# Two groups of Strassen differences, from VectorE to GpSimd, in a two-layer network

## The chip, the cores and the metric

The kernel is one program on one core of a Trainium2 chip. The metric is the device time of one execution in microseconds (us). The core has engines that run their own instruction queues and meet at semaphores: TensorE (PE in the profile; PEld is its weight load) multiplies matrices into PSUM, VectorE (DVE) does elementwise work and reductions, ScalarE (ACT) does activations, casts and copies, GpSimd (POOL) does elementwise work too, and SyncE (SP) issues the DMAs here. SBUF and PSUM are the on-chip memories; HBM holds inputs, outputs and what is put by.

## The reference

Two layers over 1024 tokens of width 1024, in float32. Layer 0 mixes tokens by sliding-window attention with sinks, layer 1 by a gated recurrence (HGRN2); each is followed by an MLP with squared ReLU and a hidden width of 4096, and a last RMS norm ends the network:

```python
for layer in range(DEPTH):
    h = rmsnorm(x, mix_norm[layer])
    y = sliding_window_attention(h, ...) if layer % 2 == 0 else hgrn2_recurrence(h, ...)
    x = x + y
    h = rmsnorm(x, mlp_norm[layer])
    x = x + jnp.square(jax.nn.relu(h @ w_up)) @ w_down
return rmsnorm(x, final_norm)
```

In layer 1 `h @ w_in` gives four projections (q, f, i, g), each 1024 x 1024.

## The kernel before

**Layout.** Activations are held transposed: 8 tiles of 128 features (`kt`), each with two halves of 512 tokens (`hf`). A tile is 128 partitions by 512 float32 columns. Tiles are named by tag: `a` (60 buffers), `t` (18), `m` (6), raw weights `wr` (6), split weights `wh` and `wl` (5 each), and the PSUM banks `p` and `q` (4 each). The profile gives these tags as names, with buffer numbers left out.

**Precise products.** Each operand of a matrix product is split into a high part, rounded to fp32r by a cast on ACT (`a<-t` or `wh<-wr`), and the rest, a subtraction on VectorE (`a<-t,a` or `wl<-wr,wh`). `mm3` (line 491) makes three matmuls of them. Both tiles of a split must be there before TensorE can use them.

**Strassen.** The first projection of a layer is computed in seven products instead of eight. With u the operand tiles of the first token half and q01, q11 those of the second half (lower and upper features), the seven operands are: 1 and 2 the halves of u (`begin`, line 647), 5 = q01 - u_j, 3 = q11, 6 = q11 - (5), 7 = q11 - q01, and 4 = u_(j+4) - (6). `finish` (line 656) makes operands 5, 3, 6, 7 and 4, four tiles each, and splits them all. The stored u tiles come back from HBM by DMA into `t` tiles (`stored`). `finish` is called three times: at the end of layer 0's attention for that layer's MLP (`mlp_second`, line 705), before the recurrence's projections (`hgrn`, line 1792), and before layer 1's MLP. Products that need operands 1 and 2 alone (`pair_first`, `two_first`) are begun ahead, so that TensorE has work while `finish` runs; after them come 5, 6, 3, 7, 4 in the MLP and 5, 6, 7, 3, 4 in the recurrence, 12 matmuls each.

**The order of the work.** Nothing is issued as it is written. `Schedule.add` records every operation with its reads, its writes, the engines that may run it and a cost for each. `order` (line 358) then runs a list scheduler over the whole program: `forward` gives each engine its operations in order, by their rank, with buffers handed out as they come free; `backward` works out from the end how late each may be, which becomes its rank; four passes are made and the one with the shortest modelled time is issued. Each engine then runs its own order strictly. The model charges latencies between engines (`LATENCY`). Elementwise operations on two tiles go through `tt` (line 470):

```python
cost = {"DVE": 70 + n * 1.04 + more, "Pool": 147 + n * 2.105}
engines = ("DVE",) if e == "any" else (e,)
```

So `"any"` means VectorE, and `"Pool"` means GpSimd, where the model charges 147 + 512 x 2.105 = 1225 ns for a tile. The model has no term for two engines that use the same memory ports. All instructions are issued through one closure, so the profile gives line 433 for every one of them and groups must be told apart by tile names and time. GpSimd has, before the change, memsets and small copies in the attention, a few small operations in the recurrence and two multiplications in the last norm.

Of the kernel before, what the change touches and what calls it, by code (L numbers as in the profile page):

```python
# [14 lines left out]
ALU = mybir.AluOpType  # L15
# [363 lines left out]
class Net:  # L379
# [276 lines left out]
    def finish(self, which, upper_first=False, keep=False):  # L656

        x, t, q01, q11 = self.b, [], [], []
        self.u3, self.u5 = [], []

        def stored(j):
            z = self.t()
            self.dma(z, self.u[j], 4 * P * TH)
            return z

        def lower():
            for j in range(HK):
                q01.append(self.gained(which, j, 1))
                t.append(stored(j))
                self.tt("any", t[j], q01[j], t[j], ALU.subtract)  # L670
                x[5].append(self.split(t[j]))
                if keep:
                    self.u5.append(self.keep(t[j]))

        def upper():
            for j in range(HK):
                q11.append(self.gained(which, j + HK, 1))
                x[3].append(self.split(q11[j]))
                if keep:
                    self.u3.append(self.keep(q11[j]))  # L680

        for part in (upper, lower) if upper_first else (lower, upper):
            part()
        for j in range(HK):
            self.tt("any", t[j], q11[j], t[j], ALU.subtract)
            x[6].append(self.split(t[j]))
        for j in range(HK):
            self.tt("any", q01[j], q11[j], q01[j], ALU.subtract)
            x[7].append(self.split(q01[j]))
        self.u4 = []  # L690
        for j in range(HK):
            z = stored(j + HK)
            self.tt("any", z, z, t[j], ALU.subtract)
            x[4].append(self.split(z))
            if keep:
                self.u4.append(self.keep(z))
        return x
# [1233 lines left out]
```

## Time and profile before

| what | value |
|---|---|
| median of 3 runs | 2050.66 us (2050.44 to 2050.85) |
| the profiled execution | 2050.68 us |
| its span, first to last instruction | 2048.9 us |
| TensorE clock granted | 0.999 of full |
| busy PE, DVE, ACT, POOL | 2037.5, 1854.9, 1306.6, 57.3 us |
| HBM read and written | 394.57 and 100.14 MB |

Busy time is the union of an engine's instruction times. Matmuls overlap each other and their ends are modelled, so a busy TensorE is not a TensorE at its peak; how many matmuls fall into a window says more. A row of a timeline has the start and the length in us, the engine, the line, the operation, the tiles it writes and reads, the shapes, how many alike are merged, and in brackets the idle time before and what ended it. A duration of a VectorE row includes some 0.08 us in which the next one already runs. Rows of the chain of waits have start, length and what the chain ran through.

### The profile page before, as it was taken

To read this page: it belongs to the slowest core of one execution; us is meant where nothing else is said; L and a number is where in the kernel's file an instruction comes from. 1 tells how busy PE (TensorE), PEld (TensorE's weight loads), DVE (VectorE), ACT (ScalarE), POOL (GpSimd) and SP (SyncE) were. 2 spreads that over 40 slices of the span, in tenths; PEclk is the share of its full clock that TensorE was granted. 3 is DMA by queue.
4 is the path that set the end of the run, shared out by engine and by line. 5 is a ranking of instruction groups with operands and counts; after the bars stand their busy time and mean duration, and the time that the engine had idled before them with its cause. 6 is when DMAs were issued, how large, how long until landed. Compare 5 with 4: busy or idle time off the path is not lost.

```text
span 2048.9 us, 36889 instructions
## 1 busy us (share of the span) xinstructions
PE 2037.5 (99%) x12300; PEld 1740.4 (85%) x12300; DVE 1854.9 (91%) x3751; ACT 1306.6 (64%) x2711; POOL 57.3 (3%) x120
## 2 busy tenths in 40 slices
PE   9999999999999999999999999999999999999998
PEld 8878888899998888888888888888889999888887
DVE  8899979899999979889988889999999899997985
ACT  7577976667675544657665556666767677544573
POOL 4030000000000000000000000000000000000000
PEclk9999999999999999999999999999999999999999
DMA  6212378788789977665777788988798788997712
GB/s 227 78 52 73 134 262 270 234 273 287 262 291 312 319 264 255 214 205 198 267 267 267 264 272 286 322 287 301 246 297 293 271 286 285 323 323 238 267 52 83
DMA packets 275407, 497.19 MB, mean 243 GB/s; under 512 B 30992, under 2 KB 36368, under 8 KB 275216
## 3 DMA queue, kind: packets, MB, share of 16 engines
q1 hardware_dynamic: 275072, 494.81, 71.6%
q8 instruction: 97, 1.59, 0.3%
q14 instruction: 94, 0.77, 0.1%
q10 hardware_dynamic: 144, 0.02, 0.0%
HBM read 394.57 MB, written 100.14 MB: 241 GB/s over the span
## 4 chain that ended last, share of the span: by engine, by line
PE 93%; DVE 4%; DMA 1%; issue 1%; ACT 0%; SPq 0%; DVEq 0%
PE p L433 50%; PE q L433 44%; DVE t L433 1%; DVE a L433 1%; DVE wl L433 1%; DMA a<-in_wg 1%; DMA a<-in_x 0%; DVE m L433 0%; DVE sm L433 0%; SPq L433 0%; DMA c<-in_sinks 0%; ACT m L433 0%; ACT a L433 0%; DVE c L433 0%; ACT t L433 0%
## 5 line engine op out<-in xcount | busy, mean ns | idle before, releaser
L433 PE MATMUL p<-a,wh 128*128 128x512 f32 (+1 forms) x2832 | 779.4, 360 | 0.3 <-DVE a L433 0.2
L433 PE MATMUL q<-a,wh 128*128 128x512 f32 x2020 | 625.5, 390 | 0.0
L433 PEld LDWEIGHTS p<-a,wh 128*128 128x128 f32 x2832 | 503.0, 189 | 79.6 <-DVE a L433 1.3
L433 PE MATMUL p<-a,wl 128*128 128x512 f32 (+1 forms) x1416 | 503.5, 358 | 0.4 <-DVE wl L433 0.4
L433 PEld LDWEIGHTS q<-a,wh 128*128 128x128 f32 x2020 | 374.9, 188 | 73.8 <-ACT a L433 0.2
L433 PE MATMUL q<-a,wl 128*128 128x512 f32 x1008 | 392.1, 389 | 0.0
L433 ACT CAST wh<-m 128x512 fp32r<-128x512 f32 (+1 forms) x354 | 213.4, 607 | 195.8 <-PE q L433 100.0
L433 ACT CAST wh<-wr 128x512 fp32r<-128x512 f32 (+1 forms) x324 | 194.9, 604 | 172.5 <-PE p L433 104.6
L433 PEld LDWEIGHTS p<-a,wl 128*128 128x128 f32 x1416 | 266.0, 189 | 38.4 <-DVE wl L433 1.1
L433 DVE TENSOR_TENSOR wl<-m,wh 128x512 fp32r<-128x512 f32 (+1 forms) x354 | 234.4, 668 | 37.5 <-ACT wh L433 31.6
L433 DVE TENSOR_TENSOR a<-t,a 128x512 fp32r<-128x512 f32 (+2 forms) x321 | 211.2, 674 | 18.8 <-PE q L433 7.8
L433 DVE TENSOR_TENSOR wl<-wr,wh 128x512 fp32r<-128x512 f32 (+1 forms) x324 | 214.3, 665 | 15.3 <-ACT wh L433 13.5
L433 DVE TENSOR_TENSOR t<-t,t 128x512 f32<-128x512 f32 (+3 forms) x376 | 218.5, 601 | 9.5 <-ACT t L433 7.1
L433 PEld LDWEIGHTS q<-a,wl 128*128 128x128 f32 x1008 | 189.3, 188 | 39.2
L433 ACT ACTIVATE t<-t 128x512 f32<-128x512 f32 x288 | 179.5, 631 | 58.7 <-DVE t L433 47.6
L433 ACT CAST a<-t 128x512 fp32r<-128x512 f32 (+1 forms) x241 | 143.2, 607 | 24.2 <-DVE t L433 9.5
L433 DVE TENSOR_TENSOR t<-t,p 128x256 f32<-128x256 f32 x288 | 115.9, 414 | 15.0 <-PE p L433 11.2
L433 PE MATMUL p<-wh,a 128*128 128x512 f32 x384 | 125.9, 397 | 0.3 <-DVE a L433 0.3
L433 DVE TENSOR_TENSOR m<-wr,wr 128x512 f32<-128x512 f32 (+1 forms) x184 | 118.8, 648 | 0.3
L433 ACT COPY t<-q 128x512 f32<-128x512 f32 (+2 forms) x174 | 95.7, 556 | 20.6 <-PE q L433 16.1
L433 DVE TENSOR_TENSOR a<-a,a 128x512 fp32r<-128x512 f32 (+2 forms) x151 | 100.8, 679 | 7.7 <-ACT a L433 3.2
L433 ACT CAST a<-a 128x512 fp32r<-128x512 f32 x136 | 82.7, 619 | 25.8 <-DVE a L433 21.8
(135 smaller groups left out, 2535.9 us busy)
## 6 DMA issues: line engine op xcount, KB each, us to landing
t<-d SPq DMA_DIRECT2D x592, 256.0 KB, 4.6
a<-d SPq DMA_DIRECT2D x318, 256.0 KB, 4.2
d<-t SPq DMA_DIRECT2D x290, 256.0 KB, 3.3
wr<-in_down SPq DMA_DIRECT2D x224, 256.0 KB, 4.2
wr<-in_up SPq DMA_DIRECT2D x172, 256.0 KB, 4.3
wr<-in_win SPq DMA_DIRECT2D x68, 256.0 KB, 4.1
d<-a SPq DMA_DIRECT2D x64, 256.0 KB, 3.3
wr<-in_wqkv SPq DMA_DIRECT2D x48, 256.0 KB, 3.0
```

The lines of the kernel that those rows point to most:

```text
L433: fn(*[place(a) for a in args], **{k: place(v) for k, v in kw.items()})
```

## The change

In `finish` the four differences that make operand 7 and the four that make operand 4 go to GpSimd instead of VectorE. Their casts, their splits, the differences of operands 5 and 6 and all else are as before; the scheduler makes its plan anew with these costs. As `finish` runs three times, 24 operations move.

```diff
             self.tt("any", t[j], q11[j], t[j], ALU.subtract)
             x[6].append(self.split(t[j]))
         for j in range(HK):
-            self.tt("any", q01[j], q11[j], q01[j], ALU.subtract)
+            self.tt("Pool", q01[j], q11[j], q01[j], ALU.subtract)
             x[7].append(self.split(q01[j]))
         self.u4 = []
         for j in range(HK):
             z = stored(j + HK)
-            self.tt("any", z, z, t[j], ALU.subtract)
+            self.tt("Pool", z, z, t[j], ALU.subtract)
             x[4].append(self.split(z))
             if keep:
                 self.u4.append(self.keep(z))
```

## The prediction

> **What bounds the kernel now.** I read the page first, then the groups by line, then the chain of waits, and last windows and timelines at the three places where the edited lines run. Two groups and the totals:
>
> ```profile
> span 2048.9 us, 36889 instructions
> PE 2037.5 (99%) x12300; PEld 1740.4 (85%) x12300; DVE 1854.9 (91%) x3751; ACT 1306.6 (64%) x2711; POOL 57.3 (3%) x120
> PE 93%; DVE 4%; DMA 1%; issue 1%; ACT 0%; SPq 0%; DVEq 0%
> ...
> L433 DVE TENSOR_TENSOR t<-t,t 128x512 f32<-128x512 f32 (+3 forms) x376 | 218.5, 601 | 9.5 <-ACT t L433 7.1 <-PE q L433 0.6
> L433 POOL TENSOR_TENSOR a<-a,t 128x512 f32<-128x512 f32 x2 | 2.6, 1302 | 689.0 <-DVE a L433 677.6 <-ACT t L433 11.4
> ```
>
> TensorE bounds the kernel (99% busy, 93% of the chain), VectorE is next at 91%, and GpSimd has nearly nothing. GpSimd has done the operation in question twice in this program: 1302 ns each. Every line has the number of one helper (L433), so the stages must be found by time. `finish` runs three times: before layer 0's MLP (300 to 332 us), before the recurrence's projections (912 to 944) and before layer 1's MLP (1418 to 1458). Windows there (length; busy time and count of PE, PEld, DVE, ACT, POOL; clock; DMA):
>
> ```profile
> 300.00:332.00 32.00, 32.00 (x147) 26.60 (x146) 31.39 (x54) 24.19 (x43) 0.00 (x0) 1.00 0.86 278
> 360.00:376.00 16.00, 16.00 (x72) 13.28 (x71) 10.13 (x20) 9.83 (x19) 0.00 (x0) 1.00 0.76 245
> 912.00:944.00 32.00, 31.76 (x144) 25.91 (x143) 31.83 (x53) 21.86 (x39) 0.00 (x0) 1.00 0.38 136
> 940.00:945.00 5.00, 4.39 (x18) 2.78 (x17) 5.00 (x9) 1.11 (x2) 0.00 (x0) 1.00 0.16 54
> 1418.00:1458.00 40.00, 40.00 (x177) 32.72 (x176) 39.53 (x67) 35.87 (x64) 0.00 (x0) 1.00 0.81 284
> ```
>
> VectorE is full in all three: 31.39 of 32, 31.83 of 32, 39.53 of 40 us. What differs is how close TensorE is behind it. In the second place it already waits. The chain of waits there, and its usual step for 12 matmuls:
>
> ```profile
> 316.14 2.72 PE p L433 x12
> ...
> 929.27 10.71 PE p L433 x48
> 939.99 0.60 DVE t L433
> 940.59 0.60 DVE wl L433
> 941.19 0.60 DVE a L433
> 941.79 0.60 DVE t L433
> 942.39 1.20 DVE a L433 x2
> 943.60 0.60 DVE t L433
> ```
>
> A matmul takes 2.72 / 12 = 0.227 us. The 18 of 940 to 945 account for 18 x 0.227 = 4.08 us, so TensorE stands idle for 0.92 us; the chain runs on VectorE because the fourth operand's splits (the two `a` at 942.39) come too late. In the other two places the last split of the fourth operand (VectorE) and the first matmul that reads it (TensorE) are these, first stage, then third:
>
> ```profile
> 331.87 0.69 DVE L433 TENSOR_TENSOR a<-t,a 128x512 fp32r<-128x512 f32 x1 [0.33 <-ACT a L433]
> 339.37 0.62 PE L433 MATMUL q<-a,wh 128*128 128x512 f32 x2
> 1456.76 0.69 DVE L433 TENSOR_TENSOR a<-t,a 128x512 fp32r<-128x512 f32 x1
> 1457.68 0.39 PE L433 MATMUL q<-a,wh 128*128 128x512 f32 x1
> ```
>
> Its reader in the first stage is the second matmul of that row, at 339.37 + 0.23 = 339.60: 7.0 us after 331.87 + 0.69 = 332.56. In the third stage 1457.68 - 1457.45 = 0.23 us are left. So VectorE has 7 us to spare in the first stage, 0.2 in the third, and none in the second.
>
> **The change part by part.** Removed from VectorE: in each stage four differences q11 - q01 for the seventh operand and four z - t for the fourth, 24 in all. Each is a `t<-t,t` over 512 columns and frees one step of VectorE's queue, 0.60 us by two consecutive rows:
>
> ```profile
> 1441.11 0.69 DVE L433 TENSOR_TENSOR a<-t,a 128x512 fp32r<-128x512 f32 x1
> 1441.71 0.69 DVE L433 TENSOR_TENSOR t<-t,t 128x512 f32<-128x512 f32 x1
> ```
>
> That is 8 x 0.60 = 4.8 us less per stage. Nothing else is removed; casts, splits, loads and TensorE's work stay, and no DMA is issued anew or past another.
>
> Added on GpSimd: 8 x 1.30 = 10.4 us per stage. Its queue is empty there (its instructions before and after the second stage):
>
> ```profile
> 853.76 0.18 POOL L433 IOTA t<- 128x64 int32 x1 [615.81 <-PE q L433]
> ...
> 993.23 0.56 POOL L433 MEMSET t<- 64x256 f32 x2 [138.69 <-ACT wh L433]
> ```
>
> So its own time is hidden if it does not touch VectorE. It does. VectorE (first five rows) beside the two GpSimd operations (last two):
>
> ```profile
> 2017.12 0.68 DVE L433 TENSOR_TENSOR a<-a,q 128x512 f32<-128x512 f32 x1
> 2017.72 1.08 DVE L433 TENSOR_TENSOR t<-t,t 128x256 f32<-128x256 f32 x1
> 2021.30 0.42 DVE L433 TENSOR_TENSOR t<-t,t 128x256 f32<-128x256 f32 x1
> 2029.92 0.69 DVE L433 TENSOR_TENSOR a<-a,q 128x512 f32<-128x512 f32 x1 [0.32 <-ACT t L433]
> 2030.52 1.02 DVE L433 TENSOR_TENSOR t<-t,t 128x256 f32<-128x256 f32 x1
> ...
> 2017.22 1.30 POOL L433 TENSOR_TENSOR a<-a,t 128x512 f32<-128x512 f32 x1 [677.60 <-DVE a L433]
> 2029.96 1.30 POOL L433 TENSOR_TENSOR a<-a,t 128x512 f32<-128x512 f32 x1 [11.44 <-ACT t L433]
> ```
>
> Alone a 256-column `t<-t,t` takes 0.42. Issued 0.50 us into GpSimd's operation it took 1.08 (0.66 longer), issued 0.56 into the other it took 1.02 (0.60 longer). Both times it was held until 1.16 us after GpSimd's start. The `a<-a,q` beside the same operations, with one input from PSUM, took its usual 0.68: only VectorE operations with both inputs in SBUF are held. So a moved difference frees 0.60 us of VectorE and holds it for up to 1.16: **+0.56 us** where the next operation reads two SBUF tiles. Where it reads PSUM, that one slips through and the balance is 1.16 - 0.60 - 0.60 = -0.04. The first and last PSUM readers in the second stage (6 of 53 operations) and in the third (9 of 67):
>
> ```profile
> 912.26 0.68 DVE L433 TENSOR_TENSOR m<-p,a 128x512 f32<-128x512 f32 x1
> 938.71 1.28 DVE L433 TENSOR_TENSOR t<-p,t 128x512 f32<-128x512 f32 x2
> 1418.90 0.68 DVE L433 TENSOR_TENSOR m<-p,a 128x512 f32<-128x512 f32 x1
> 1457.96 0.69 DVE L433 TENSOR_TENSOR t<-q,t 128x512 f32<-128x512 f32 x1
> ```
>
> About one in eight, so of eight moved operations seven cost 0.56 and one gains 0.04: 3.9 us per stage.
>
> The Trainium skill, SBUF — State Buffer, section Who interferes with whom, says that a VectorE instruction with two SBUF inputs contends with a GpSimd instruction that reads SBUF, and that whoever starts first holds the ports for the whole instruction. By that the hold would be the full 1.30 us, 0.70 per operation, 4.8 us per stage, and the sum would come to 2059.6. The rows show 1.16.
>
> The sum by stage. First: 3.9 us late against 7 us of slack, and VectorE makes it up in 360 to 376, where it is idle for 16 - 10.13 = 5.9 us: 0. Cover: that slack; if it were gone, +3.9. Second: TensorE already waits on VectorE, so all of it: +3.9. Third: 3.9 less 0.47 us of idle VectorE (40 - 39.53) less 0.2 of slack: +3.2. Together +7.1.
>
> Bounds of the hold, which decides: at the low end GpSimd reads in gaps and VectorE loses nothing. Then VectorE gains 4.8 us per stage, but TensorE only the 0.92 us for which it stands still in the second: -0.9. At the high end the whole 1.30 us of GpSimd's row, and every held operation loses a step of its own besides (0.60): 1.30 per moved operation, 10.4 per stage, 20.8 less 0.7 in the two that count: +20. I take 1.16, which both rows give for this very operation.
>
> The added waits: ACT's casts of both operands now wait for GpSimd, and behind them in ACT's order stand copies out of PSUM. One GpSimd operation that also waits for VectorE's step is 1.30 + 0.60 = 1.9 us, four in a row 7.6. In the second stage the sixth operand's last difference, which the fourth's needs, is this one:
>
> ```profile
> 923.66 0.68 DVE L433 TENSOR_TENSOR t<-t,t 128x512 f32<-128x512 f32 x1
> ```
>
> So the fourth's can begin about 924.3 and end about 932, while TensorE waits for their splits at 942: 10 us are there for cast and split, and I add nothing for ACT.
>
> The profiled execution took 2050.68 us (span 2048.9 and 1.8 around it), the median is 2050.66. Sum: 2050.7 + 7.1 = **2057.8**.
>
> **The rivals.** *A, relief:* GpSimd and VectorE alternate without loss, or the differences run early where VectorE is not yet full. For it: four of the eight could start in the less dense start of each stage. Against: both rows of the contention, and windows full from 912 and from 1418 on. It decides if the hold is below 0.60 us. Time: 2050.7 - 0.9 = 2049.8, not slower. The Trainium skill, Perfetto Trace Analysis, section Optimizing Scalar/DVE Operations, says that a saturated VectorE may be worth relieving, even onto GpSimd, and warns in the same place of the shared port; the rows speak for the warning.
>
> *B, GpSimd late:* in-order casts behind GpSimd hold up ACT's copies out of PSUM, so that TensorE waits for banks too. It decides if a moved operation takes over 4 us instead of 1.9 (16 us from 924 would eat the 10). Price: one more chain of 7.6 us in one stage: about 2065. Against it: the empty GpSimd queue.
>
> *C, another plan:* engines' orders come from a list scheduler that books 1.22 us on GpSimd and knows no hold; it plans the whole program anew with a freer VectorE, and TensorE's small waits elsewhere may shrink or grow. For a gain over 0.2% it must find 4.1 us plus the 7.1: unlikely if the hold is real, but with a hold near nothing 4.2 us beyond the 0.9 give 2045.6. Against: TensorE's idle time in the whole span is 2048.9 - 2037.5 = 11.4 us.
>
> **How the numbers follow.** 0.2% of 2050.7, about what a measurement of this kernel can tell from no change, is 4.1 us: slower begins at 2054.8, faster below 2046.6. Forecast (2053 to 2062, mostly above 2054.8) 0.58; A 0.22; B 0.08; C 0.12. Slower: 0.52 of the forecast, B and 0.02 of C make 0.62. Same: the forecast's low end 0.06, A 0.22: 0.28. Faster: 0.10 of C. The range leaves out C's gains and the far side of B: 2047.5 to 2065. The likeliest case's own is 2053 to 2062.
>
> **What would show it.** In the changed profile GpSimd has 26 such operations near 1.3 us, 24 of them in the three stages. VectorE's two-SBUF-input rows beside them take up to 1.8 us instead of 0.69, while rows with `p` or `q` among the inputs keep 0.69. TensorE has no new wait in the first stage; in the second and third the chain runs through VectorE for some 3 to 5 us more. The forecast is wrong if rows beside GpSimd keep 0.69, if TensorE's loss is in the first stage or behind the third, or if GpSimd itself ends the wait.

## The result, and the profile after

The changed kernel takes 2070.03 us (median; 2069.16 to 2071.93) against 2050.66 us for the kernel before on the same chip: 1.0094 times as long, with an interval of 1.0084 to 1.0105. It is slower by 19.4 us, where 7.1 were forecast. The totals of its page:

```profile
span 2068.2 us, 36892 instructions
PE 2043.8 (99%) x12300; PEld 1743.3 (84%) x12300; DVE 1866.0 (90%) x3727; ACT 1303.9 (63%) x2711; POOL 99.0 (5%) x144
...
L433 DVE TENSOR_TENSOR t<-t,t 128x512 f32<-128x512 f32 (+3 forms) x352 | 209.9, 618 | 12.2 <-ACT t L433 9.7
```

VectorE has 24 instructions fewer than before (3727 against 3751) and yet 11.1 us more busy time (1866.0 against 1854.9). TensorE stands idle for 2068.2 - 2043.8 = 24.4 us, 13.0 more than before; its busy time has grown by 6.3 us too, though its 12300 matmuls are the same.

GpSimd's new operations by group, and VectorE's timeline with GpSimd's beside it, in the first stage:

```profile
L433 POOL TENSOR_TENSOR t<-t,t 128x512 f32<-128x512 f32 x24 | 40.2, 1689 | 230.3 <-DVE t L433 80.6 <-DMA d<-a 79.7 <-ACT t L433 65.3
```

```profile
302.80 0.69 DVE L433 TENSOR_TENSOR t<-t,t 128x512 f32<-128x512 f32 x1 [0.19 <-ACT t L433]
303.45 1.74 DVE L433 TENSOR_TENSOR a<-t,a 128x512 fp32r<-128x512 f32 x1
305.12 1.78 DVE L433 TENSOR_TENSOR t<-t,t 128x512 f32<-128x512 f32 x1
306.82 0.68 DVE L433 TENSOR_TENSOR a<-t,a 128x512 fp32r<-128x512 f32 x1
...
302.85 3.50 POOL L433 TENSOR_TENSOR t<-t,t 128x512 f32<-128x512 f32 x2 [3.16 <-ACT t L433]
```

Beside two GpSimd operations that follow each other, one VectorE row per operation takes 1.74 and 1.78 us in place of 0.69. In the three stages 23 VectorE rows with two SBUF inputs exceed 0.9 us, by 21.8 us in sum over 0.69. Five rows with one input in PSUM lay beside a GpSimd operation, two of them issued inside it; the longest took 0.685. GpSimd pays as well: 1.69 us for one on average, against 1.30 before.

Windows at the places of the prediction, with the columns as there:

```profile
300.00:332.00 32.00, 29.78 (x136) 24.47 (x135) 31.60 (x45) 20.31 (x37) 11.52 (x6) 1.00 0.79 252
360.00:376.00 16.00, 16.00 (x72) 13.27 (x71) 10.20 (x19) 8.78 (x15) 0.00 (x0) 1.00 0.77 252
912.00:944.00 32.00, 28.11 (x124) 22.14 (x122) 29.52 (x37) 20.53 (x37) 12.29 (x8) 1.00 0.37 133
946.00:951.00 5.00, 5.00 (x16) 4.23 (x16) 4.14 (x11) 0.83 (x2) 0.00 (x0) 0.50 0.15 54
1418.00:1458.00 40.00, 37.21 (x157) 30.28 (x156) 38.53 (x53) 23.97 (x40) 11.81 (x8) 0.96 0.80 279
```

All three stages have lost matmuls, the first as well: 136 of 147, 124 of 144 and 157 of 177 are left. After the second stage there is a stretch of 5 us in which TensorE never waits, runs 16 matmuls (30 in the same window before, small ones counted in both), and has a granted clock of 0.50.

TensorE's rows with the waits, first, second and third stage:

```profile
331.37 0.73 PE L433 MATMUL q<-a,wh 128*128 128x512 f32 x2 [2.22 <-ACT t L433]
335.54 0.72 PE L433 MATMUL q<-a,wh 128*128 128x512 f32 x2 [1.16 <-ACT t L433]
340.58 0.73 PE L433 MATMUL q<-a,wh 128*128 128x512 f32 x2 [0.87 <-ACT t L433]
...
938.20 0.50 PE L433 MATMUL p<-a,wh 128*128 128x512 f32 x1 [0.47 <-DVE a L433]
942.02 0.73 PE L433 MATMUL p<-a,wh 128*128 128x512 f32 x2 [1.72 <-ACT t L433]
945.43 1.87 PE L433 MATMUL q<-c,t 128*128 128x1 f32 x8 [2.44 <-DVE t L433]
947.16 1.20 PE L433 MATMUL p<-a,wh 128*128 128x512 f32 x2
...
1442.21 0.73 PE L433 MATMUL q<-a,wh 128*128 128x512 f32 x2 [2.79 <-DVE m L433]
1443.80 1.05 PE L433 MATMUL q<-a,wh 128*128 128x512 f32 x2
1461.48 0.50 PE L433 MATMUL q<-a,wh 128*128 128x512 f32 x1 [1.45 <-DVE a L433]
1462.59 0.73 PE L433 MATMUL q<-a,wh 128*128 128x512 f32 x2 [0.38 <-ACT t L433]
```

In the first stage every wait ends on a ScalarE copy (`t`), in the others mostly on VectorE. The rows at 947.16 and 1443.80 are merged pairs that take 1.20 and 1.05 us where 0.62 is usual.

To compare versions, a stage's loss is how much longer than in the kernel before TensorE needs from the stage's first matmul to the first matmul of the part behind it (in the kernel before 313.0 to 401.0, 917.1 to 972.2 and 1330.9 to 1725.6 us). "Slow matmuls" is what runs of three or more matmuls of 512 columns took beyond 0.227 us each, at some 0.43 us one. All of these are worked out from TensorE's rows, in one profiled execution of each version. The 0.8 us of slow matmuls of the version "new plan, GpSimd only writes" and 0.6 of the 2.8 of the planner's lie at the program's start, 5.5 us into the span, and not in the stages.

| version | time, us | ratio (interval) | loss, stage 1 | 2 | 3 | slow matmuls |
|---|---|---|---|---|---|---|
| the change | 2070.03 | 1.0094 (1.0084 to 1.0105) | 5.2 | 8.3 | 7.8 | 3.0 |
| new plan, differences on VectorE | 2061.79 | 1.0053 (1.0038 to 1.0068) | 2.1 | 6.5 | 4.6 | 1.6 |
| old plan, differences on GpSimd | 2063.71 | 1.0064 (1.0049 to 1.0079) | 4.6 | 5.2 | 4.2 | 2.4 |
| new plan, GpSimd only writes | 2048.07 | 0.9986 (0.9977 to 0.9996) | 0.1 | -1.4 | -0.7 | 0.8 |
| old plan, GpSimd only writes | 2050.26 | 0.9997 (0.9988 to 1.0006) | 0.0 | -0.7 | 0.2 | 0 |
| planner books the hold | 2061.06 | 1.0050 (1.0034 to 1.0067) | 0.6 | 2.2 | 7.5 | 2.8 |
| seventh operand only | 2057.59 | 1.0032 (1.0020 to 1.0045) | 1.9 | 3.0 | 4.2 | 2.6 |
| fourth operand only | 2058.89 | 1.0039 (1.0024 to 1.0054) | 1.9 | 3.8 | 3.0 | 1.4 |
| half the columns | 2055.70 | 1.0024 (1.0015 to 1.0034) | 1.7 | 0.8 | 3.5 | 0 |
| square root put off | 2070.15 | 1.0092 (1.0077 to 1.0107) | 5.6 | 7.5 | 8.0 | 5.9 |
| two copies first | 2073.37 | 1.0110 (1.0093 to 1.0127) | 6.7 | 7.5 | 7.9 | 5.5 |
| three copies first | 2068.60 | 1.0090 (1.0073 to 1.0107) | 3.0 | 8.3 | 7.0 | 1.6 |

The new plan also starts the first stage 1.5 us sooner than the old one, so the change's three losses, 21.3 us, exceed its 19.4.

### The profile page after: what moved, and what is told of

Read it like the earlier page. It is cut to its first block, busy times and chain, and to the rows that moved or that the text cites. A ratio compares the mean times of both kernels' runs of the same rounds, so it can differ in the third digit from the quotient of the medians.

```text
span 2068.2 us, 36892 instructions
## 1 busy us (share of the span) xinstructions
PE 2043.8 (99%) x12300; PEld 1743.3 (84%) x12300; DVE 1866.0 (90%) x3727; ACT 1303.9 (63%) x2711; POOL 99.0 (5%) x144
## 5 line engine op out<-in xcount | busy, mean ns | idle before, releaser
L433 DVE TENSOR_TENSOR a<-t,a 128x512 fp32r<-128x512 f32 (+1 forms) x321 | 217.3, 697 | 18.2 <-PE q L433 7.6
L433 DVE TENSOR_TENSOR t<-t,t 128x512 f32<-128x512 f32 (+3 forms) x352 | 209.9, 618 | 12.2 <-ACT t L433 9.7
```

Of the source, the lines that this page charges most:

```text
L433: fn(*[place(a) for a in args], **{k: place(v) for k, v in kw.items()})
```

## The experiments: is it the hold?

The "hold" is the time for which a GpSimd operation keeps a VectorE instruction from going on. Three theories stand in the expectations. H: GpSimd's reads hold VectorE. P: the new order of work is bad, whoever makes the differences. G: GpSimd itself is late, and ScalarE's casts wait for it.

**GpSimd only writes.** The changed kernel's plan is kept. At the place of each of the 24 differences GpSimd runs two memsets of the output instead, without reads; the differences are left out.

```diff
             self.tt("Pool", q01[j], q11[j], q01[j], ALU.subtract)
+            self.s.ops[-1].instead = self.written(q01[j])
...
+    def written(self, out):
+        steps = [self.call(self.nc.gpsimd.memset, out, 0.0)[0] for _ in range(2)]
```

> The changed kernel with its own plan, but each of the 24 GpSimd differences is replaced by two GpSimd memsets of the same output tile (the differences for operands 7 and 4 are left out), which read no SBUF. GpSimd is occupied about as long. Theory H: no hold, the plan's assumption comes true: 2048.5 to 2050.5. Theory P: 2070. Theory G: the memsets end about as late as the differences would without contention, so 2050 if only the contention makes them late and 2060 or more if the order of GpSimd does.

It took 2048.07 us, 0.4 under the range of theory H and far from P's 2070. The totals of its page, and the memsets by group:

```profile
span 2045.4 us, 36908 instructions
PE 2036.2 (100%) x12300; PEld 1740.2 (85%) x12300; DVE 1843.7 (90%) x3727; ACT 1303.1 (64%) x2711; POOL 82.2 (4%) x168
```

```profile
L433 POOL MEMSET t<- 128x512 f32 x48 | 24.5, 527 | 208.8 <-DVE t L433 172.5 <-DMA t<-d 26.9 <-issue 7.8
```

The same 3727 VectorE instructions in the same order take 1843.7 us in place of 1866.0: GpSimd's reads cost VectorE 22.3 us, and the program 2070.03 - 2048.07 = 22.0. The memsets (2 x 0.53 = 1.06 us per place) hold nothing. The Trainium skill, SBUF — State Buffer, section Who interferes with whom, says just this: a VectorE instruction with two SBUF inputs contends with a GpSimd instruction that reads SBUF, and not with one that only writes it. So the whole loss comes with GpSimd's reads, and the new plan without them is a little faster than the old (-2.5 us).

The memsets also need no inputs and are done sooner than the differences, so this run alone does not part theory H from G. The changed kernel's trace does: ScalarE's casts wait for GpSimd three times, 2.1 us in all, and no wait of VectorE or TensorE ends on GpSimd.

**One operand, or half the columns.** Three more versions keep the plan and take away part of GpSimd's reads. Two put the memsets at the place of one operand's differences only. The third keeps both operands on GpSimd but works on 256 of the 512 columns.

```diff
             self.tt("Pool", z, z, t[j], ALU.subtract)
+            self.s.ops[-1].instead = self.call(self.nc.gpsimd.tensor_tensor, z[:, : TH // 2], z[:, : TH // 2], t[j][:, : TH // 2], ALU.subtract)[0]
```

> The changed kernel with its own plan; GpSimd makes the seventh operand's 12 differences, and the fourth's 12 are left out and replaced by two GpSimd memsets each, which read nothing. Theory H: 12 holds of 1.16 us, half of the 22 us between the plan with memsets (2048.1) and the changed kernel (2070.0): about 2059. If only the fourth operand's late differences hurt: about 2050.

> The changed kernel with its own plan; GpSimd makes the fourth operand's 12 differences, and the seventh's 12 are left out and replaced by two GpSimd memsets each. Theory H: the other half, about 2059, so that the two halves add up to the 22 us. If a late fourth operand hurts by itself, because TensorE needs it last: over 2064.

> The changed kernel with its own plan, but each GpSimd difference covers only the first 256 of 512 columns (the other half is left out). The same number of operations, half of the reading. Theory H with a hold that follows the reading: 0.6 us each, 14 us of holds, about 2059. If each GpSimd operation has a fixed price whatever its size: near 2068.

The seventh operand alone costs 2057.59 - 2048.07 = 9.5 us more than writing only, the fourth alone 10.8, together 20.3 of the 22.0: the two nearly add up, and neither is the culprit. With half the columns GpSimd's operation takes 1.14 us on average, hardly more than the two memsets; 18 VectorE rows are held by 9.3 us in sum, and the cost over writing only is 7.6. That is under the expected 2059, which reckoned with 14 us of holds, and far from the 2068 of a fixed price per operation: over the four versions the cost follows the time held (21.8, 10.7, 10.4 and 9.3 us held cost 22.0, 9.5, 10.8 and 7.6).

```profile
L433 POOL TENSOR_TENSOR t<-t,t 128x256 f32<-128x256 f32 x24 | 27.0, 1135 | 232.5 <-ACT t L433 151.3 <-DVE t L433 66.8 <-DVE wl L433 13.2
```

## The experiments: the freed time and the plan

**The plan alone, and the move alone.** One version keeps the changed kernel's plan but issues the 24 differences on VectorE, at their places in it; the other keeps the plan of the kernel before and issues them on GpSimd, by the same line with `gpsimd` for `vector`. The cut is of the first.

```diff
-            op.ways[op.engine][0]()
+            (op.instead or op.ways[op.engine][0])()
...
+            self.s.ops[-1].instead = self.call(self.nc.vector.tensor_tensor, z, z, t[j], ALU.subtract)[0]
```

> The plan made for the changed kernel, kept as it is, but the 24 differences are issued on VectorE at their places in that plan. GpSimd reads nothing, so no hold; VectorE has 24 x 0.60 = 14.4 us of work that the plan did not count. Theory H (each GpSimd difference holds VectorE for 1.16 us, and the new plan has already spent the 0.60 us that each move frees): the 27.8 us of holds cost 19.4, so 8.4 us are absorbed, and here 14.4 - 8.4 = 6 us are lost: about 2056.7. Theory P (the new order itself is bad, whoever does the differences): still about 2070. Theory G (GpSimd is late and ScalarE waits behind it): about 2051.

> The plan of the kernel before, kept as it is, but the 24 differences are issued on GpSimd at their places in it. Theory H: each moved operation costs VectorE 1.16 - 0.60 = 0.56 us net, nothing is spent elsewhere, so the sum of the prediction should hold: 2054 to 2060. Theory P: the old order is good, so 2050 to 2052. Theory G: GpSimd's share comes as late as in the changed kernel or later, since here it stands where VectorE had it, so 2065 or more.

The move under the old plan costs 2063.71 - 2050.6 = 13.1 us; the new plan adds 2070.03 - 2063.71 = 6.3. The new plan with the work back on VectorE costs 11.2 without any hold: it was drawn up for a VectorE with 14.4 us less to do, and it has little room for them. Both runs missed what theory H made of them. The first lost 11.2 us and not 6; the second came out at 2063.71, above the 2054 to 2060 of the prediction's own sum and below G's 2065. Theory P's values (2070, and 2050 to 2052) are further off, and so is G's 2051 for the first.

**The freed time by itself.** The plan of the kernel before, with the two memsets in the place of each difference: VectorE is freed and not held.

```diff
             self.tt("any", z, z, t[j], ALU.subtract)
+            self.s.ops[-1].instead = self.written(z)
```

> The plan of the kernel before, and in it each of the 24 differences is replaced by two memsets of the same output on GpSimd; the differences are left out, so operands 7 and 4 are zero. VectorE is freed of 24 x 0.60 = 14.4 us and not held. Beside it stands the same plan with the real GpSimd operations, 2063.7 us with 23.3 us of held rows. Theory S (freed time cannot be cashed by TensorE, which stood idle for little, but under the old plan it is slack that absorbs a part of the holds; the new plan has spent that slack on other VectorE work): 2047.5 to 2050, so 23.3 us of holds cost 14 to 16 here and 22 under the new plan. Rival T (freed and held time simply add on TensorE's path): 2063.7 - 23.3 = 2040.4, between 2039 and 2043.

2050.26 us: 0.4 less than before, within the interval of no change. Its windows at the three stages show where the freed time is:

```profile
300.00:332.00 32.00, 32.00 (x147) 26.60 (x146) 27.27 (x45) 24.25 (x44) 0.00 (x0) 1.00 0.86 277
912.00:944.00 32.00, 32.00 (x146) 26.28 (x144) 27.91 (x46) 21.48 (x39) 8.09 (x16) 1.00 0.39 139
1418.00:1458.00 40.00, 40.00 (x177) 32.94 (x176) 36.22 (x60) 36.15 (x66) 7.07 (x14) 1.00 0.85 297
```

VectorE idles for 4.7, 4.1 and 3.8 us in them, and TensorE is full: nothing on TensorE's side can take the time up. So the 14.4 us of differences cost 0.4 us on VectorE under the old plan, and 11.2 under the new one. But under the old plan the freed time is slack that absorbs holds. There GpSimd's reads raise VectorE's busy time from 1842.3 (the totals of this run) to 1864.9 (the old plan with the real differences), 22.6 us, and the time by 2063.71 - 2050.26 = 13.45. Under the new plan 22.3 us of it cost 22.0. Theory S holds, a quarter of a microsecond outside its range and with a price of the holds slightly under its 14 to 16; theory T is 10 us off.

```profile
PE 2036.6 (99%) x12300; PEld 1740.4 (85%) x12300; DVE 1842.3 (90%) x3727; ACT 1306.3 (64%) x2711; POOL 81.2 (4%) x168
```

```profile
PE 2042.3 (99%) x12300; PEld 1741.8 (84%) x12300; DVE 1864.9 (90%) x3727; ACT 1305.9 (63%) x2711; POOL 97.0 (5%) x144
```

**A planner that knows.** The scheduler books 1160 ns on VectorE whenever it places a two-input operation on GpSimd.

```diff
             op.begin, free_at[e] = t, t + cost
+            if e == "Pool" and op.two:
+                free_at["DVE"] = max(free_at["DVE"], t) + HOLD
```

> The changed kernel, but the scheduler books 1160 ns on VectorE whenever it places a two-input GpSimd operation, so the plan knows the hold. Theory H: the loss falls to VectorE's net surplus where it is full, as the prediction summed it: 2054 to 2060. Theory P: any value, since it is another plan. Theory G: unchanged, about 2070, since GpSimd's own booking is the same.

2061.06 us: 9.0 us of the 19.4 come back, nearly all in the first two stages (0.6 and 2.2 lost in place of 5.2 and 8.3). The third still loses 7.5, 2.2 of it in slow matmuls; why this plan does no better there was not followed up. The time is 1.1 us above the 2054 to 2060 that theory H gave it, and still slower than leaving the differences on VectorE.

## The experiments: the first stage

The prediction put the first stage at nothing, and its waits end on ScalarE. ScalarE's timeline there, changed kernel:

```profile
330.12 0.20 ACT L433 ACTIVATE sm<-sm 128x4 f32<-128x4 f32 x1 [3.90 <-DVE sm L433]
330.23 0.60 ACT L433 CAST wh<-m 128x512 fp32r<-128x512 f32 x1
330.74 0.58 ACT L433 COPY t<-q 128x512 f32<-128x512 f32 x1
334.39 0.62 ACT L433 CAST wh<-m 128x512 fp32r<-128x512 f32 x1 [3.07 <-PE q L433]
334.91 0.58 ACT L433 COPY t<-q 128x512 f32<-128x512 f32 x1
```

The two copies empty the PSUM banks for which TensorE waits at 331.37 and 335.54. Their matmuls had ended 4.3 and 5.8 us earlier; the copies stood in ScalarE's queue behind a square root and a cast whose inputs VectorE had yet to make.

**The square root put off**, with the small chain behind it, by 40 ScalarE operations:

```diff
         self.tt("DVE", self.square[hf], y, y, ALU.mult, 4)
+        if hf and not self.layer:
+            for op in self.s.ops[-6:]:
+                op.put_off = True
```

> The changed kernel with its own plan, but in the first stage the square root on ScalarE that waits for VectorE's small operation on the second token sum, and the five small VectorE operations behind it, are issued 40 ScalarE operations later. Theory Q (in the first stage TensorE waits for copies out of PSUM that stand in ScalarE's queue behind this square root, which a late VectorE holds up): the first stage loses 2.4 us less or nearly so, the wait before the third product of the first pair goes, and the time is about 2067.5. Theory D (TensorE waits there for VectorE's splits themselves): no change in the stage, 2069.5 to 2070.5.

2070.15 us, no change: theory Q's 2067.5 did not come, and the time is theory D's. TensorE's waits in the stage fell from 4.7 us to 3.7 (1.08 and 2.62), since the next cast in the queue waited for VectorE as well; and 1.6 us of slow matmuls behind the longer of the two took the gain.

**Two copies first, then three.** With the square root put off, the two copies are issued ahead of the cast in front of each; in the second version a third copy also goes ahead of a cast and two squarings. Apart from the small chain, all engines but ScalarE keep their order.

```diff
+            i = act.index(copy)
+            if act[i - 1].cast:
+                act[i - 1 : i + 1] = act[i], act[i - 1]
```

> Only the first stage is edited. ScalarE's square root is put off as in the run before, and besides, the two copies out of PSUM of the first pair of products (COPY t<-q at 330.74 and 334.91 in the changed kernel's profile, whose matmuls had been done 4.3 and 5.8 us earlier) are issued ahead of the casts wh<-m that stood in front of them and waited for VectorE. Theory H (a held VectorE reaches TensorE through ScalarE's queue, where copies out of PSUM stand behind an operation that waits for VectorE): the first stage's loss of 5.2 us falls to 1 to 2, and the time to 2066 to 2067.5. Rival V (TensorE waits for VectorE's splits themselves, the copies only look like it): 2069 to 2071, unchanged, with the gaps in the first stage turned into waits for w tiles. Rival L (what the first stage gains is lost again in the later ones, because nothing else is bound there): under half of the gain is left, about 2068.

> As the run before, in the first stage, with two differences: the copy out of PSUM of the third product (COPY t<-q, in the run before at 341.50, its matmuls done at 337.3) is issued ahead of the cast and the two squarings that stood in front of it (CAST wh<-m at 337.97, the four ACTIVATE t<-t at 339.12, which wait for VectorE); and the rest of the program is issued in the changed kernel's own order, so the attention's wait of 0.98 us at 186.15 of that run does not come. Theory H (in the first stage VectorE's lateness reaches TensorE through copies out of PSUM that stand in ScalarE's queue behind operations that wait for VectorE; with two copies freed, the third took over the whole wait of 4.96 us): the sum of TensorE's waits in the first stage falls from 4.7 to 1 to 2 us, and the time to 2065.5 to 2067.5. Rival V (the lateness reaches TensorE by whatever way is left, the next splits of weights included): the waits stay near 4.7 us in sum and the time at 2069 to 2071.

With two copies first the time is 2073.37 us, slower than any of the three theories had it (2066 to 2071). TensorE ran through the places of the first two waits and then stood at the third copy for all of it. TensorE's rows, and ScalarE's, of that run:

```profile
336.71 0.61 PE L485 MATMUL q<-a,wh 128*128 128x512 f32 x2
342.12 1.03 PE L485 MATMUL q<-a,wh 128*128 128x512 f32 x2 [4.80 <-ACT t L485]
342.94 0.63 PE L485 MATMUL q<-a,wl 128*128 128x512 f32 x1
```

```profile
339.12 2.47 ACT L485 ACTIVATE t<-t 128x512 f32<-128x512 f32 x4 [0.53 <-DVE t L485]
341.50 0.57 ACT L485 COPY t<-q 128x512 f32<-128x512 f32 x1
```

One wait of 4.96 us (from the time a matmul should have begun) has taken the place of three that sum to 4.73, and the long wait is followed by nine slow matmuls (1.7 us). This version also reaches the stage 1.6 us later than the changed kernel, with a wait of 0.98 us before 187.59 in the attention that the other does not have; the later start and the slow matmuls together are its 3.3 us. With the third copy freed as well, 2068.60 us, TensorE's waits are these:

```profile
337.85 0.74 PE L489 MATMUL q<-a,wh 128*128 128x512 f32 x2 [1.00 <-ACT t L489]
345.90 0.73 PE L489 MATMUL q<-a,wh 128*128 128x512 f32 x2 [0.68 <-ACT t L489]
```

With one more, before 353.34, they are 2.5 us in place of 4.7, and the stage loses 3.0 in place of 5.2. The theory of the copies held for 2.2 us, less than it expected (a fall to 1 to 2 us), by one profiled execution of each version. The time's median fell by 1.4 only, short of its 2065.5 to 2067.5, and the runs overlap (2068.36 to 2069.96 against 2069.16 to 2071.93); this version starts the stage 1.1 us later, and has no slow matmuls in the third stage where the changed kernel has 1.4 us of them. So the fall of the waits is shown, and a gain in time is not. How the other 2.5 us of waits come about was not taken apart.

## Why the prediction was right in direction and wrong in size

- **What bounds the kernel**: right. TensorE bounds it, and VectorE's lateness is what reaches it.
- **The hold**: right. It was put at 1.16 us per operation where the next VectorE step reads two SBUF tiles, 21 times in 24 (24.4 us); 23 rows were held, by 0.95 us on average, 21.8 us in sum. PSUM readers slipped by, as said; the prediction's two rows could not show this, since they had begun before GpSimd's operations (2017.12 against 2017.22, 2029.92 against 2029.96), but those issued inside one in the changed kernel (932.87 and 1433.97, 0.68 us) do. The rule of the Trainium skill, SBUF — State Buffer, section SBUF: two separate sides, of a hold for the whole instruction (1.30 by GpSimd's row) was no nearer. (By that rule the prediction's stage is 7 x 0.70 + 0.10 = 5.0 us and not 4.8, and its 2059.6 would be 2060.0.)
- **The credit of 0.60 us per freed step**: the first step that failed, as the prediction took it from the old plan's queue and used it, with that plan's slack, for a plan made anew. On the old plan it nearly holds: the sum for the second and third stage, 3.9 and 3.2, stands beside 5.2 and 4.2 measured, 1.2 of the 5.2 being slow matmuls. On the new plan the freed time is already spent (the same work put back on VectorE costs 11.2 us there), and the stages lose 8.3 and 7.8. The plan's part is 6.3 us in all.
- **The first stage, put at 0 behind 7.0 us of slack**: the second step that failed; 5.2 (4.6 under the old plan). The slack was that of VectorE's last split against its matmul. It left out the other way from VectorE to TensorE, by ScalarE's queue, in which copies out of PSUM stand behind casts of what VectorE makes. The three copies, issued first with the square root put off, account for 2.2 us of it; by which way the other 3.0 come is open. "I add nothing for ACT" was the same oversight, made for casts and splits alone.
- **TensorE's clock** was no term of the sum. The runs of slow matmuls cost 3.0 us, and the token sums at 945.43 took 1.87 us instead of the usual 0.95: 3.9 together. That fits the granted clock, 0.997 in place of 0.999 of 2068 us (4.1), as far as three digits tell.
- **The rivals**: A (relief) would have needed time that TensorE can use, and there is little (2050.26 under the old plan and 2048.07 under the new one, with all of it freed and nothing held). B's time of 2065 is nearer than the forecast. Its condition did not come: GpSimd's operations took 1.69 us on average, the longest 2.80, not over 4. But the second half of its way did, copies out of PSUM held up behind casts in ScalarE's queue, with VectorE as the late engine in place of GpSimd. C's new plan was real, with the opposite sign: it gains 2.5 us without holds, and costs 6.3 with them.
- **The signs named**: two-SBUF rows of up to 1.8 us, found (1.79); GpSimd's rows near 1.3 us, wrong (1.69); no new wait in the first stage, wrong; 3 to 5 us in each of the others, right on the old plan only.

The terms together: 7.1 forecast, 6.0 for what the sum lacked under the old plan (the first stage's 4.6 and 2.3 in the other two, less 0.9 by which the stages' sum exceeds the run's median), and 6.3 for the new plan make the 19.4.

## What to carry to other kernels

Before work goes from VectorE to GpSimd, see whether it reads SBUF beside VectorE instructions with two SBUF inputs: here each moved operation then held VectorE for 0.95 us to free 0.60, and the freed time by itself was worth 0.4 us under the old plan and 2.5 under a new one, because TensorE had little idle time to give. Slack has to be measured on every way to the bounding engine, in-order queues of third engines included. Where a scheduler plans anew with a cost that leaves the contention out, it spends the freed time as if it were there, so that slack read from the old plan no longer covers anything.

## What the runs showed of the hardware that was not expected

TensorE's clock can fall after waits of under 3 us. After the wait of 2.79 us before 1442.21, 1.6 us of matmuls ran at the usual pace, and then seven took 0.43 us each; the granted clock is 0.50 from 1443.6 to 1447.0. In the second stage, after waits of 1.72 and 2.44 us, it is 0.50 from 945.3 to 952.1, and eight matmuls of 512 columns cost 1.6 us more.

The length of the wait does not decide this alone, as rows of the version with three copies first (L489) and of that with the square root put off (L443) show:

```profile
1441.31 0.73 PE L489 MATMUL q<-a,wh 128*128 128x512 f32 x2 [2.71 <-DVE m L489]
1442.11 0.62 PE L489 MATMUL q<-a,wh 128*128 128x512 f32 x2
1443.49 0.61 PE L489 MATMUL q<-a,wh 128*128 128x512 f32 x2
...
1461.24 0.50 PE L443 MATMUL q<-a,wh 128*128 128x512 f32 x1 [1.45 <-DVE a L443]
1462.36 0.84 PE L443 MATMUL q<-a,wh 128*128 128x512 f32 x2 [0.38 <-ACT t L443]
1463.42 1.06 PE L443 MATMUL q<-a,wh 128*128 128x512 f32 x2
```

The 2.22 us before 331.37 had no such sequel, nor had 2.71 us before 1441.31 in the version with three copies first. In the version with the square root put off, two waits of 1.45 and 0.38 us, before 1461.24 and 1462.36, were followed by 1.4 us of slow matmuls; the changed kernel has the same two waits, before 1461.48 and 1462.59, and no slow matmul behind them. So from these runs a wait cannot be given a price: what followed one of 1.3 to 2.8 us lay between nothing and 2.6 us. That several short waits are cheaper than a long one is seen once (4.73 us in three waits without slow matmuls, 4.96 us in one with 1.7 us of them) and is not shown as a rule.

The Trainium skill, TensorE: Matmul & The Clock Gate, Part 1, gives half rate after an idle window of some 3.4 us. Half rate is what these rows show, but here 2.79 us of idle time were enough.

GpSimd's hold reached it in turn: VectorE and GpSimd took turns, and GpSimd's 512 columns took 1.69 us in place of 1.30.
